# A residual between two layers: squares taken by the scalar engine on transposed rows, and the last three projection tiles run by token halves

## The chip, the cores and the metric

The kernel runs on one core of a Trainium2 chip. The core has a matmul engine (TensorE, PE), a vector engine (VectorE, DVE), a scalar engine (ScalarE, ACT), a general engine (GpSimd, POOL) and a queue engine (SyncE, SP) that issues most of the transfers. Each engine works through its own list of instructions in order; semaphores tie the lists together. The metric is the time of one execution in microseconds (us), smaller is better.

## The reference

Two layers over 528 tokens (16 learned tokens ahead of 512) of width 2048, in float32. Layer 0 is softmax attention, layer 1 gated linear attention (GLA). Around both stands the same frame:

```python
for i in range(DEPTH):                       # DEPTH = 2
    y = rmsnorm(h, pre_norm[i])
    if i % N_MIXERS == 0:
        y = attention_mixer(y, attn_w_in[j], ..., attn_w_out[j], ...)
    else:
        y = gla_mixer(y, gla_w_in[j], gla_gk_up[j], gla_gk_bias[j], gla_o_norm[j], gla_w_out[j])
    h = h + rmsnorm(y, post_norm[i])

def rmsnorm(x, w):
    y = x * rsqrt(mean(x * x, axis=-1) + 1e-6)
    return y * w
```

The change lies between the layers: the output projection of layer 0 (`attn_w_out`), its norm, the residual sum `h + ...`, the norm ahead of layer 1, and the first products of layer 1.

## The kernel before, in words

**Layout.** In this stretch, activations lie transposed: 16 row tiles of 128 features, each with all 528 tokens (T) along the row. Each float32 matmul is made of three cheaper ones: activations and weights are split into a high and a low part (`uh`, `ul`; `whi`, `wlo`), and `three` (L154 to L156) multiplies high by high, low by high and high by low. `split` takes the high part on ACT (L131) and the low part on DVE (L132). Tokens come in two halves of 264 (`HALVES`).

**Weights.** `weights` loads 1024 columns by 128 rows (512 KB) into one of two buffers `wraw`, and splits them into one of three pairs `whi`, `wlo`. A load waits until the split two before it has read its `wraw` buffer; a split waits until PE has used the pair three before it. `project` computes one output tile of 128 features from two such pieces, one token half after the other, each with 16 x 3 matmuls. `group` runs several output tiles at once, contraction step by contraction step, so that it can begin while its input is still being made.

**The stretch.** (1) A `group` computes output tiles 0 and 1 of layer 0's projection while the attention's last rows arrive. Beside it, the weights of GLA's low-rank gate are brought in: `wr` (loaded on POOL's queue, split into `wl`) and `ur`, which has a buffer of its own and is copied into the rows of `ups`. (2) `project` computes tiles 2 to 15. For each half, `squares` takes the output to `hs` (times `post_norm`) and its square on ACT; POOL adds the squares into `acc` (L648). (3) After tile 15, `mean_rsqrt` sums `acc` over the features by a matmul with ones, and makes the scale `r0` (DVE, then a logarithm and an exponential on ACT), per half. (4) `residual(k, a, b)` does row tile k: DVE multiplies `hs` by `r0` (L669), the old `h` (`h0`, reloaded on SP's queue) is added by DVE for even and POOL for odd k (L670), ACT casts the high part times `pre_norm` to `uh` (L671), DVE makes `ul` (L672), ACT squares the new `h` (L677), POOL adds that into `acc` (L678). (5) The next `group` (key tiles of GLA, accumulated in four PSUM banks) calls `low_rank` at each step: that does one residual ahead, multiplies the row tile by `wl` (L691, L692, tile `plr`), transposes it (L698, tile `ht`), copies it (L700, tile `hb`) and stores it for the end of the kernel. The first six row tiles (`NB`) go by halves, the rest whole. (6) `mean_rsqrt` makes the second norm `r1row` from `acc`; it scales what was accumulated (`lt`, `kf`); five transposes turn it into a column `r1col`.

**What sets the order.** The code keeps a model clock (`Clock`): every matmul steps it, and work handed to `clk.after` is written out when the clock gets there. The lists of the engines are then laid out by the framework from that order; weights are drawn ahead (`high_priority`).

Of the kernel before, what the change touches and what calls it, by code (L numbers as in the profile page):

```python
# [82 lines left out]
def hybrid_encoder(  # L83
# [59 lines left out]
    def weights(src, ahead=AHEAD, queue=nc.sync):  # L143
        n = src.shape[-1]
        with tc.high_priority(ahead):
            raw = wpool.tile([P, 1024], F32, tag="wraw", name="wraw", bufs=2)
# [2 lines left out]
            queue.dma_start(out=raw.rearrange("p (k n) -> p k n", n=n), in_=src)
# [480 lines left out]
    nc.gpsimd.dma_start(out=ur, in_=gla_gk_up[0].rearrange("d r n -> r d n"))  # L630
    for t in lrs + [ups]:
        G.memset(t.bitcast(F32), 0.0)
    A.copy(ups[0:16], ur)
# [1 line left out]
    V.tensor_tensor(ups[32:48], ur, ups[0:16].bitcast(F32), op=ALU.subtract)
# [4 lines left out]
    def squares(m, ps, a, b):  # L640
        A.activation(hs[m][:, a:b], ps, AF.Copy, scale=col(POST + m))
        if m == 0:
            A.activation(acc[:, a:b], ps, AF.Square)  # L643
# [20 lines left out]
    def residual(k, a, b):  # L664
        if a == 0:
            h0s[k] = t2.tile([P, T], F32, tag="h0", name="h0", bufs=6)
            nc.sync.dma_start(out=h0s[k], in_=h0_d[k])
# [1 line left out]
        V.tensor_tensor(h, h, r0[:, a:b], op=ALU.mult)  # L669
        (G if k % 2 else V).tensor_tensor(h, h, h0s[k][:, a:b], op=ALU.add)  # L670
        A.activation(hi, h, AF.Copy, scale=col(PRE + KT + k))  # L671
        V.scalar_tensor_tensor(ul[:, k, a:b], h, col(PRE + KT + k), hi.bitcast(F32), op0=ALU.mult, op1=ALU.subtract)  # L672
        if k == 0:
            A.activation(acc[:, a:b], h, AF.Square)
        else:
            sq = t2.tile([P, T], F32, tag="sq1", name="sq1")[:, :b - a]
# [1 line left out]
            G.tensor_tensor(acc[:, a:b], acc[:, a:b], sq, op=ALU.add)  # L678
# [9 lines left out]
    def low_rank(k, part):  # L688
# [4 lines left out]
        if part == 0:  # L693
            return
        ps = (ps_p.tile([P, 512], F32, tag="pp", name="ht") if k % 2 else
              ps_t.tile([P, 512], F32, tag="t", name="ht"))
        for t in range(4):
            PE.transpose(ps[:, t * P:(t + 1) * P], hs[k][:, t * P:(t + 1) * P], ident)  # L698
        hb = t2.tile([P, 512], F32, tag="hb", name="hb")
        A.copy(hb, ps)  # L700
        nc.sync.dma_start(out=h1_d[:, :, k * P:(k + 1) * P].rearrange("t p c -> p t c"),
                            in_=hb.rearrange("p (t c) -> p t c", t=4))
# [31 lines left out]
    lt = tp.tile([P, T], F32, name="lt")  # L734
    for ps, a, b in plr:
        V.tensor_tensor(lt[:, a:b], ps, r1row[:, a:b], op=ALU.mult)
    for i, ps, a, b in banks1:
        take_k(i, ps, a, b)
# [371 lines left out]
```

## Time and profile before

| what | us |
|---|---|
| median of three runs (lowest, highest) | 1824.53 (1823.79, 1826.96) |
| the profiled execution | 1824.21 |
| its span, from first to last instruction | 1822.2 |
| PE busy | 1787.3 (98%) |
| DVE busy | 1014.2 (56%) |
| ACT busy | 891.2 (49%) |
| POOL busy | 204.7 (11%) |

Matmuls overlap, so PE's busy time says only where it had nothing to do. Times in the rows are from the span's start; the stretch of the change lies between about 750 and 1030. In rows, `out<-in` names the tiles, `x2` merges neighbours, and a square bracket gives the idle time ahead of an instruction and who ended it.

### The profile page before, as it was taken

The page shows a single profiled execution, that of the slowest core. Times are in us where ns is not written, and L with a number is a line of the kernel's source. Part 1 is how long each engine was busy: PE and PEld are TensorE (multiplying, and loading weights), DVE is VectorE, ACT ScalarE, POOL GpSimd, SP SyncE. Part 2 cuts the span into 40 slices and gives each one's busy share as a digit, 9 for nine tenths or more (in the row PEclk, how much of TensorE's full clock was granted, in tenths as well). Part 3 has the DMA queues.
Part 4 walks back from the last instruction along what each step waited for, and adds up shares of the span by engine and source line. Part 5 has one row for each costly group of instructions (what it writes and reads, how often), then busy time and mean ns, then how long its engine had stood idle before and what let it go on. Part 6 is the DMA issues. An engine that isn't in the chain of part 4 may idle for free.

```text
span 1822.2 us, 31830 instructions
## 1 busy us (share of the span) xinstructions
PE 1787.3 (98%) x12838; PEld 1685.5 (92%) x12838; DVE 1014.2 (56%) x1942; ACT 891.2 (49%) x1836; POOL 204.7 (11%) x215
## 2 busy tenths in 40 slices
PE   8999999999999999999997999999999999999998
PEld 8899999999999999999987898998999899988886
DVE  5776565656565657622258475656456565654224
ACT  4554544445454545533345586556447554743221
POOL 3211111111111010211137000000000000000000
PEclk9999999999999999999998999999999999999999
DMA  8322323232323332533335323232232333434333
GB/s 268 105 70 74 90 84 87 87 88 84 92 82 91 87 116 81 182 86 93 93 89 162 87 72 90 83 82 82 81 93 76 87 91 88 135 116 167 99 93 127
DMA packets 265955, 184.22 MB, mean 101 GB/s; under 512 B 8188, under 2 KB 241984, under 8 KB 265280
## 3 DMA queue, kind: packets, MB, share of 16 engines
q1 hardware_dynamic: 261152, 165.78, 31.6%
q0 software_dynamic: 4656, 16.42, 2.5%
q8 instruction: 100, 1.64, 0.4%
q14 instruction: 47, 0.39, 0.1%
HBM read 156.03 MB, written 19.64 MB: 96 GB/s over the span
## 4 chain that ended last, share of the span: by engine, by line
PE 91%; DVE 3%; DMA 2%; ACT 1%; issue 1%; POOL 1%; SPq 0%; DVEq 0%; POOLq 0%; ACTq 0%
PE pp L154 22%; PE pp L156 22%; PE pp L155 22%; PE f L1024 2%; PE f L1022 2%; PE f L1023 2%; PE pT L492 2%; PE s L473 1%; PE s L474 1%; PE s L475 1%; PE o L512 1%; PE o L513 1%; PE o L902 1%; PE o L901 1%; PE o L900 1%
## 5 line engine op out<-in xcount | busy, mean ns | idle before, releaser
L154 PE MATMUL pp<-uh,whi 128*128 128x264 f32 (+1 forms) x3072 | 927.2, 302 | 0.7 <-ACT acc L643 0.4
L156 PE MATMUL pp<-uh,wlo 128*128 128x264 f32 (+1 forms) x3072 | 916.5, 298 | 0.3 <-POOL wlo L279 0.3
L155 PE MATMUL pp<-ul,whi 128*128 128x264 f32 (+1 forms) x3072 | 915.0, 298 | 1.2 <-DVE ul L340 1.2
L154 PEld LDWEIGHTS pp<-uh,whi 128*128 128x128 f32 x3072 | 578.1, 188 | 19.6 <-issue 0.8
L155 PEld LDWEIGHTS pp<-ul,whi 128*128 128x128 f32 x3072 | 578.8, 188 | 17.4 <-DVE ul L340 1.8
L156 PEld LDWEIGHTS pp<-uh,wlo 128*128 128x128 f32 x3072 | 578.3, 188 | 16.9 <-POOL wlo L279 0.6
L132 DVE TENSOR_TENSOR wlo<-wraw,whi 128x1024 fp32r<-128x1024 f32 (+1 forms) x257 | 315.5, 1228 | 384.5 <-ACT whi L131 379.2
L131 ACT CAST whi<-wraw 128x1024 fp32r<-128x1024 f32 (+1 forms) x257 | 267.4, 1042 | 416.6 <-PE pp L155 297.1
L482 ACT ACTIVATE pn<-s,mx 128x528 f32<-128x528 f32 (+1 forms) x72 | 50.3, 698 | 88.5 <-DVE mx L479 62.7
L1024 PE MATMUL f<-whi,ul 128*128 128x512 f32 x192 | 75.6, 394 | 0.0
L1022 PE MATMUL f<-whi,uh 128*128 128x512 f32 x192 | 75.5, 393 | 0.0
L1023 PE MATMUL f<-wlo,uh 128*128 128x512 f32 x192 | 75.3, 392 | 0.0
L225 POOL TENSOR_TENSOR qw<-qw,cos 128x528 f32<-128x528 f32 x24 | 31.8, 1327 | 371.5 <-DMA qs<-qw 314.5
L927 POOL DMA_DIRECT2D og_d<-og x24 | 12.9, 543 | 487.2 <-DVE og L925 487.2
L478 DVE TENSOR_REDUCE mx<-s 128x1 f32<-128x528 f32 (+1 forms) x72 | 50.7, 705 | 18.7 <-PE s L475 17.5
L497 DVE TENSOR_TENSOR pl<-pT,ph 128x512 fp32r<-128x512 f32 (+1 forms) x80 | 47.4, 592 | 4.8 <-ACT ph L496 3.8
L235 DVE TENSOR_TENSOR qw<-qw,qs 128x528 f32<-128x528 f32 x24 | 17.0, 707 | 59.1 <-POOL qs L226 59.1
L496 ACT CAST ph<-pT 128x512 fp32r<-128x512 f32 (+1 forms) x80 | 40.6, 507 | 16.0 <-PE pT L492 10.0
L467 POOL TENSOR_TENSOR gs<-gs,gr 128x528 f32<-128x528 f32 x16 | 21.1, 1322 | 220.9 <-ACT gs L141 204.1
L1023 PEld LDWEIGHTS f<-wlo,uh 128*128 128x128 f32 x192 | 36.1, 188 | 8.3
L1024 PEld LDWEIGHTS f<-whi,ul 128*128 128x128 f32 x192 | 36.0, 188 | 8.3
L1022 PEld LDWEIGHTS f<-whi,uh 128*128 128x128 f32 x192 | 36.1, 188 | 8.1
(310 smaller groups left out, 2750.6 us busy)
## 6 DMA issues: line engine op xcount, KB each, us to landing
wraw<-in_gla_w_in_dram SPq DMA_DIRECT2D x96, 512.0 KB, 3.8
wraw<-in_attn_w_in_dram SPq DMA_DIRECT2D x94, 512.0 KB, 3.8
wraw<-in_attn_w_out_dram SPq DMA_DIRECT2D x32, 512.0 KB, 3.9
wraw<-in_gla_w_out_dram SPq DMA_DIRECT2D x32, 512.0 KB, 3.8
qs<-qw SPq DMA_DIRECT2D x96, 66.0 KB, 2.8
h<-h_d SPq DMA_DIRECT2D x16, 264.0 KB, 3.5
h_d<-h POOLq DMA_DIRECT2D x16, 256.0 KB, 3.4
h_d<-hb SPq DMA_DIRECT2D x16, 256.0 KB, 2.8
```

Of the source, the lines that this page charges most:

```text
L131: A.copy(hi, src)
L132: V.tensor_tensor(lo, src, hi.bitcast(F32), op=ALU.subtract)
L154: PE.matmul(ps, wh, uh[:, k, a:b], start=first, stop=False)
L155: PE.matmul(ps, wh, ul[:, k, a:b], start=False, stop=False)
L156: PE.matmul(ps, wl, uh[:, k, a:b], start=False, stop=last)
L478: V.reduce_max(mx, s, axis=AX.XY)
L482: A.activation(pn[:, :T].rearrange("p (a b) -> p a b", a=2), s, AF.Exp, bias=mx, scale=SCALE, accum_out=sm)
L496: A.copy(ph[:, :, c:c + m], pt[:, :, qc:qc + m])
L497: V.tensor_tensor(pl[:, :, c:c + m], pt[:, :, qc:qc + m], ph[:, :, c:c + m].bitcast(F32), op=ALU.subtract)
L1022: PE.matmul(ps, uh[:, k, ts], wh[:, kk], start=(k == 0), stop=False)
L1023: PE.matmul(ps, uh[:, k, ts], wl[:, kk], start=False, stop=False)
L1024: PE.matmul(ps, ul[:, k, ts], wh[:, kk], start=False, stop=(k == KT - 1))
```

## The change

- POOL takes no part in the residual any more: DVE makes all sums with `h0`, and the sum of squares for the second norm comes from ACT. `token_major` transposes four row tiles for 128 tokens into one bank, lets ACT square it with a sum along the row (into `s1`), and for the 512 real tokens copies it and stores it. Tokens now lie on the partitions, so the second norm is a column `r1col` from `s1`; it is spread into `r1row` by five matmuls of ones with a scaled identity (`second_norm`).
- The last three tiles of the projection (`TAIL`) run for token half 1 first and then for half 2, with the same split weights (`kept`; three of the six pieces lie in buffers `own`).
- The residuals of half 1 are put beside the tail's second half (`residuals`), those of half 2 into the group; ten row tiles go by halves in the group. `h0` is loaded by halves into five buffers.
- `ur` loses its own buffer: it is loaded in two parts into the weights' two `wraw` buffers.

The diff, cut to its core:

```diff
-    def weights(src, ahead=AHEAD, queue=nc.sync):
+    def weights(src, ahead=AHEAD, queue=nc.sync, own=None):
...
-    ur = tp.tile([16, 2, 1024], F32, name="ur")
-    nc.gpsimd.dma_start(out=ur, in_=gla_gk_up[0].rearrange("d r n -> r d n"))
     for t in lrs + [ups]:
         G.memset(t.bitcast(F32), 0.0)
-    A.copy(ups[0:16], ur)
-    A.copy(ups[64:80], ur)
-    V.tensor_tensor(ups[32:48], ur, ups[0:16].bitcast(F32), op=ALU.subtract)
+    for d in range(2):
+        ur = wpool.tile([P, 1024], F32, tag="wraw", name="ur", bufs=2)[:16]
+        nc.gpsimd.dma_start(out=ur, in_=gla_gk_up[0, d])
+        A.copy(ups[0:16, d], ur)
+        A.copy(ups[64:80, d], ur)
+        V.tensor_tensor(ups[32:48, d], ur, ups[0:16, d].bitcast(F32), op=ALU.subtract)
...
     def residual(k, a, b):
-        if a == 0:
-            h0s[k] = t2.tile([P, T], F32, tag="h0", name="h0", bufs=6)
-            nc.sync.dma_start(out=h0s[k], in_=h0_d[k])
+        h0 = t2.tile([P, HALF], F32, tag="h0", name="h0", bufs=5)
+        nc.sync.dma_start(out=h0, in_=h0_d[k][:, a:b])
...
-        (G if k % 2 else V).tensor_tensor(h, h, h0s[k][:, a:b], op=ALU.add)
+        V.tensor_tensor(h, h, h0, op=ALU.add)
...
-        if k == 0:
-            A.activation(acc[:, a:b], h, AF.Square)
-        else:
-            sq = t2.tile([P, T], F32, tag="sq1", name="sq1")[:, :b - a]
-            A.activation(sq, h, AF.Square)
-            G.tensor_tensor(acc[:, a:b], acc[:, a:b], sq, op=ALU.add)
...
+        if part != 0 and k % 4 == 3:
+            for i, t in enumerate((2, 3, 4)):
+                clk.after(1.2 + 0.8 * i, lambda t=t: token_major(k - 3, t))
...
+    def token_major(k, t):
+        _, c, n = TOK[t]
+        turn[0] += 1
+        ps = (ps_p.tile([P, 512], F32, tag="pp", name="ht") if turn[0] % 2 and spare[0] else
+              ps_t.tile([P, 512], F32, tag="t", name="ht"))[:n]
+        for j in range(4):
+            PE.transpose(ps[:, j * P:(j + 1) * P], hs[k + j][:, c:c + n], ident)
+        hb = t2.tile([P, 512], F32, tag="hb", name="hb")[:n]
+        A.activation(hb, ps, AF.Square, accum_out=s1[:n, t, k // 4:k // 4 + 1])
+        if t < 4:
+            A.copy(hb, ps)
+            nc.sync.dma_start(out=h1_d[t][:, k * P:(k + 4) * P], in_=hb)
...
-                clk.after(1.5, lambda: mean_rsqrt(r0, [acc[:, a:b], sq], a, b))
-                clk.after(2.5, lambda: ahead(NA))
+                clk.after(2.0, lambda: mean_rsqrt(r0, [acc[:, a:b], sq], a, b))
+                clk.after(3.5, lambda: side.append(clk.drive(residuals())))
...
-    NA, NB = 2, 6
+    TAIL, NB = 3, 10
...
+    def residuals():
+        for k in range(KT):
+            ahead(1)
+            yield 0.6
+            if k % 4 == 3:
+                for t in range(2):
+                    clk.after(2.0 + t, lambda k=k, t=t: token_major(k - 3, t))
+            yield 0.6
...
-    for m in range(2, KT):
+    for m in range(2, KT - TAIL):
         project(w_out0, m * P, HALVES, evac)
+    kept = {}
+    for part in HALVES:
+        for m in range(KT - TAIL, KT):
+            if m not in kept:
+                kept[m] = [weights(w_out0[:, k0:k0 + 8, m * P:(m + 1) * P], own=own.pop(0) if own else None)
+                           for k0 in (0, 8)]
+            project(w_out0, m * P, (part,), evac, ws=kept[m])
...
-    for a, b in HALVES:
-        mean_rsqrt(r1row, [acc[:, a:b]], a, b)
+    def second_norm():
+        V.reduce_sum(r1col, s1, axis=AX.X)
+        V.tensor_scalar(r1col, r1col, 1.0 / D, EPS, op0=ALU.mult, op1=ALU.add)
+        rsqrt_inplace(r1col)
+        for t, c, n in TOK:
+            dg = t2.tile([P, P], F32, tag="dg", name="dg")
+            V.tensor_scalar(dg, ident, r1col[:, t:t + 1], None, op0=ALU.mult)
+            ps = ps_t.tile([P, 512], F32, tag="t", name="mrow")[:, :n]
+            PE.matmul(ps, ones, dg[:, :n], start=True, stop=True)
+            A.copy(r1row[:, c:c + n], ps)
...
+    clk.after(5.0, second_norm)
...
-    for t, c, n in TOK:
-        ps = ps_t.tile([P, 512], F32, tag="t", name="rt")[:n, :P]
-        PE.transpose(ps, r1row[:, c:c + n], ident)
-        V.tensor_copy(r1col[:n, t:t + 1], ps[:, 0:1])
```

Three places show what moves. First POOL's list around the end of layer 0's attention, before the change (`gs` is the gate of the last head, `lr` and `ups` are cleared here):

```order
L467 TENSOR_TENSOR gs<-gs,gr 128x528 x2
L624 DMA wr<-in_gla_w_in_dram 128x16x32
L626 MEMSET wl 128x2048
L630 DMA ur<-in_gla_gk_up_dram 16x2x1024
L632 MEMSET lr_9780 80x528
L632 MEMSET lr_9781 80x528
L632 MEMSET ups 80x2048
```

and with it:

```order
L467 TENSOR_TENSOR gs<-gs,gr 128x528
L633 DMA ur<-in_gla_gk_up_dram 16x1024
L467 TENSOR_TENSOR gs<-gs,gr 128x528
L633 DMA ur<-in_gla_gk_up_dram 16x1024
L630 MEMSET lr_9780 80x528
L624 DMA wr<-in_gla_w_in_dram 128x16x32
L626 MEMSET wl 128x2048
L630 MEMSET lr_9781 80x528
L630 MEMSET ups 80x2048
```

Both `ur` loads, which wait for a `wraw` buffer, now stand ahead of `wr` and the clearing of `wl`. Second, ACT's list at the same place, before (`whi` are splits of weights, `h` and `acc` the evacuation of the first output tile):

```order
L131 CAST whi<-wraw 128x1024
L131 CAST wl<-wr 128x16x16 x2
L131 CAST whi<-wraw 128x1024
L633 CAST ups<-ur 16x2048
L634 CAST ups<-ur 16x2048
L641 ACTIVATE h_9791<-pp,cols 128x264
L643 ACTIVATE acc<-pp 128x264
L131 CAST whi<-wraw 128x1024
```

and with the change:

```order
L131 CAST wl<-wr 128x16x16 x2
L634 CAST ups<-ur 16x1024
L635 CAST ups<-ur 16x1024
L634 CAST ups<-ur 16x1024
L635 CAST ups<-ur 16x1024
L131 CAST whi<-wraw 128x1024
L642 ACTIVATE h_9791<-pp,cols 128x264
L644 ACTIVATE acc<-pp 128x264
L642 ACTIVATE h_9791<-pp,cols 128x264
L131 CAST whi<-wraw 128x1024
```

The two splits for output tile 2, which stood ahead of and between the gate's casts, come after them, the first right behind, the second two evacuations later. Third, DVE's list inside the group of layer 1, before (the numbers tell the row tiles `h` and the buffers of `h0` apart, `r_9808` is `r0`):

```order
L669 TENSOR_TENSOR h_9797<-h_9797,r_9808 128x528
L672 SCALAR_TENSOR_TENSOR ul<-h_9794,cols,uh 128x264
L670 TENSOR_TENSOR h_9797<-h_9797,h_11733 128x528
L672 SCALAR_TENSOR_TENSOR ul<-h_9795,cols,uh 128x264
L672 SCALAR_TENSOR_TENSOR ul<-h_9796,cols,uh 128x264
L669 TENSOR_TENSOR h_9798<-h_9798,r_9808 128x528
L672 SCALAR_TENSOR_TENSOR ul<-h_9797,cols,uh 128x528
L669 TENSOR_TENSOR h_9799<-h_9799,r_9808 128x528
```

and with it, at the start of half 2:

```order
L672 SCALAR_TENSOR_TENSOR ul<-h_9805,cols,uh 128x264
L669 TENSOR_TENSOR h_9791<-h_9791,r_9808 128x264
L669 TENSOR_TENSOR h_9792<-h_9792,r_9808 128x264
L670 TENSOR_TENSOR h_9791<-h_9791,h_11680 128x264
L672 SCALAR_TENSOR_TENSOR ul<-h_9806,cols,uh 128x264
L670 TENSOR_TENSOR h_9792<-h_9792,h_11694 128x264
L669 TENSOR_TENSOR h_9793<-h_9793,r_9808 128x264
L672 SCALAR_TENSOR_TENSOR ul<-h_9791,cols,uh 128x264
```

The sums of every row tile are on DVE's list now, all rows are halves, and half 1 is through (its last row tile is 9806) when half 2 begins.

More of the change, by code (lines that the diff above doesn't have):

```diff
@@ L146, in weights @@
             raw = wpool.tile([P, 1024], F32, tag="wraw", name="wraw", bufs=2)
-            hi = wpool.tile([P, 1024], F32R, tag="whi", name="whi")
-            lo = wpool.tile([P, 1024], F32R, tag="wlo", name="wlo")
+            hi, lo = own or (wpool.tile([P, 1024], F32R, tag="whi", name="whi"),
+                             wpool.tile([P, 1024], F32R, tag="wlo", name="wlo"))
             queue.dma_start(out=raw.rearrange("p (k n) -> p k n", n=n), in_=src)
@@ L644, in squares @@
             return
-        sq = t2.tile([P, 512], F32, tag="sq", name="sq")[:, :b - a]
+        sq = t2.tile([P, HALF], F32, tag="sq", name="sq")
         A.activation(sq, ps, AF.Square)
@@ L692, in low_rank @@
             PE.matmul(ps, wl[:, k, :], ul[:, k, a:b], start=False, stop=(k == KT - 1))
[L693 to L702, printed above, removed]
+        if part != 0 and k % 4 == 3:
+            for i, t in enumerate((2, 3, 4)):
+                clk.after(1.2 + 0.8 * i, lambda t=t: token_major(k - 3, t))
+    s1 = tp.tile([P, 5, 4], F32, name="s1")
+    V.memset(s1, 1.0)
+    def token_major(k, t):
[10 more added lines that the diff above has]
+            nc.sync.dma_start(out=h1_d[t][:, k * P:(k + 4) * P], in_=hb)
+    turn, spare = [0], [True]
     def evac(ps, a, b):
@@ L706, in evac @@
             if a == 0:
-                clk.after(1.5, lambda: mean_rsqrt(r0, [acc[:, a:b], sq], a, b))
-                clk.after(2.5, lambda: ahead(NA))
-            else:
-                clk.after(0.9, lambda: mean_rsqrt(r0, [acc[:, a:b], sq], a, b))
-    NA, NB = 2, 6
-    h0s = {}
-    tasks = [(k, a, b) for a, b in HALVES for k in range(NB)] + [(k, 0, T) for k in range(NB, KT)]
+                clk.after(2.0, lambda: mean_rsqrt(r0, [acc[:, a:b], sq], a, b))
+                clk.after(3.5, lambda: side.append(clk.drive(residuals())))
+            else:
+                clk.after(1.6, lambda: mean_rsqrt(r0, [acc[:, a:b], sq], a, b))
+    TAIL, NB = 3, 10
+    side = []
+    tasks = [(k, a, b) for a, b in HALVES for k in range(KT)]
     def ahead(n):
@@ L719, in ahead @@
                 residual(*tasks.pop(0))
-    for m in range(2, KT):
-        project(w_out0, m * P, HALVES, evac)
+    def residuals():
[6 more added lines that the diff above has]
+            yield 0.6
+    own = [[tp.tile([P, 1024], F32R, name=f"own{i}{w}") for w in "hl"] for i in range(3)]
+    for m in range(2, KT - TAIL):
+        project(w_out0, m * P, HALVES, evac)
+    kept = {}
[5 more added lines that the diff above has]
+            project(w_out0, m * P, (part,), evac, ws=kept[m])
+    clk.finish(*side)
     group([(w_in1, 1024, 256)], accs1, low_rank, halves=NB)
-    for a, b in HALVES:
-        mean_rsqrt(r1row, [acc[:, a:b]], a, b)
+    spare[0] = False
     def take_k(i, ps, a, b):
@@ L732, in take_q @@
         V.scalar_tensor_tensor(qf[:, i, a:b], ps, 1.0 / 16, r1row[:, a:b], op0=ALU.mult, op1=ALU.mult)
[L734 to L738, printed above, removed]
+    lt = r0
+    def second_norm():
[8 more added lines that the diff above has]
+            A.copy(r1row[:, c:c + n], ps)
+        for ps, a, b in plr:
+            V.tensor_tensor(lt[:, a:b], ps, r1row[:, a:b], op=ALU.mult)
+        for i, ps, a, b in banks1:
+            take_k(i, ps, a, b)
+    clk.after(5.0, second_norm)
     project(w_in1, 0, REAL, lambda ps, a, b: take_q(0, ps, a, b))
```

4 lines of the change are left out of this document (2 added, 2 removed).

## The prediction

> **What bounds the kernel now.** I read the page first: TensorE (PE) is busy for 98% of the span, so only its holes can be won. Its row of forty slices shows one broad hole, slices 20 to 22, which is the residual between the layers. Then I read the busy time of each engine by stage (columns: from:to, us, then PE, weight load, DVE, ACT and POOL busy with instruction counts, granted clock, DMA share, GB/s):
>
> ```profile
> 930.00:940.20 10.20, 10.20 (x82) 10.00 (x80) 2.91 (x5) 3.26 (x7) 1.47 (x2) 1.00 0.19 56
> 940.20:1003.20 63.00, 47.11 (x326) 43.85 (x325) 55.81 (x58) 34.86 (x67) 44.93 (x35) 0.92 0.51 148
> 1003.20:1027.00 23.80, 23.80 (x104) 17.47 (x103) 10.88 (x23) 8.73 (x16) 0.00 (x0) 1.00 0.33 88
> ```
>
> Before 940.2 (the projection's end) and after 1003.2 (the group's end) PE has no gap. Between them it is idle for 15.9 us and its clock averages 0.92. What would the stage take without waits? The timeline of PE gives the step from one batch of four transposes (L698) to the next, first where a step holds 8 matmuls (one token half), then where it holds 16; the last two rows are waits:
>
> ```profile
> 954.46 0.60 PE L698 MATMUL ht<-ident,h 128*128 128x128 f32 x4
> 955.90 0.60 PE L698 MATMUL ht<-ident,h 128*128 128x128 f32 x4
> ...
> 998.89 0.60 PE L698 MATMUL ht<-ident,h 128*128 128x128 f32 x4
> 1001.30 0.60 PE L698 MATMUL ht<-ident,h 128*128 128x128 f32 x4
> ...
> 969.57 0.80 PE L698 MATMUL ht<-ident,h 128*128 128x128 f32 x4 [4.42 <-ACT hb L700]
> 991.40 1.11 PE L698 MATMUL ht<-ident,h 128*128 128x128 f32 x4 [2.87 <-ACT hb L700]
> ```
>
> The steps are 1.44 and 2.41 us, so 8 matmuls take 0.97 and a batch of transposes 0.47. The stage has ten steps of 16, six of 8 with a batch and six without: 24.1 + 8.6 + 5.8 = 38.5, and with four matmuls of the first norm, at 8 matmuls' rate and double passes about 0.8, 39.3 us. The excess is 63.0 - 39.3 = 23.7 us. The waits of PE name its cause:
>
> ```profile
> PE ht L698 <- ACT hb L700: 8.2, 4, 4.4
> PE plr L692 <- DVE ul L672: 5.9, 7, 1.5
> ```
>
> ACT had itself been waiting there, for the sums of DVE and POOL. DVE is the bound: it has no pause from 946 to 996 (first row, by stage), but its operations are stretched (rows by line give ns min/median/max and both shapes; then pieces of the timelines):
>
> ```profile
> 946.00:996.00 50.00, 35.87 (x247) 33.28 (x247) 50.00 (x50) 29.13 (x54) 40.12 (x29) 0.91 0.52 152
> ...
> L669 DVE TENSOR_TENSOR h<-h,r x22: 417/697/1839, 937.7 to 985.3; 128x264 f32<-128x264 f32 x12, 128x528 f32<-128x528 f32 x10
> L672 DVE SCALAR_TENSOR_TENSOR ul<-h,cols,uh x22: 480/968/1830, 940.5 to 993.0; 128x264 fp32r<-128x264 f32 x12, 128x528 fp32r<-128x528 f32 x10
> ...
> 935.26 0.61 PE L660 MATMUL ssq<-acc,ones 128*128 128x264 f32 x2
> 937.73 0.78 DVE L669 TENSOR_TENSOR h<-h,r 128x264 f32<-128x264 f32 x2 [0.95 <-ACT r L136]
> 940.46 0.89 DVE L672 SCALAR_TENSOR_TENSOR ul<-h,cols,uh 128x264 fp32r<-128x264 f32 x2
> ...
> 962.41 3.57 DVE L669 TENSOR_TENSOR h<-h,r 128x528 f32<-128x528 f32 x2
> 961.89 1.76 POOL L670 TENSOR_TENSOR h<-h,h 128x528 f32<-128x528 f32 x1 [0.99 <-DVE h L669]
> 963.62 1.80 POOL L678 TENSOR_TENSOR acc<-acc,sq 128x528 f32<-128x528 f32 x1
> ```
>
> Two products of 528 columns took 3.57 us just where POOL ran two of its own for 1.76 and 1.80; two of 264 columns with POOL idle took 0.78.
>
> **The change, part by part.**
>
> 1. *POOL leaves the residual* (its sums of squares and half of the additions). Per half tile DVE then does two sums and one fused operation. Back to back these cost 0.78 - 0.42 = 0.36 twice and 0.89 - 0.48 = 0.41: 1.13 us, or 1.32 if none overlaps. Thirty-two halves make 36 to 42 us instead of the 50 of 946 to 996 that the old share took.
>
> 2. *The last three tiles run first for token half 1, then for half 2.* The first norm of half 1 is ready 4.5 us after its last tile (935.26 to 937.73 is 2.5 behind the norm's matmuls, which are put 2.0 later), while PE still has 3 x 48 matmuls = 17.4 us, one norm and four batches of transposes ahead: 20.0 us. So DVE works for 15.5 us under a full PE; before, it had about 2.5 (937.73 to 940.2).
>
> Call the end of half 1 zero. DVE: 16 halves x 1.13 = 18.1, three weight splits x 1.22 = 3.7, two remaining POOL additions that may block 0.76 each = 1.5: half 1 done at 27.8. The second norm's scale costs about a microsecond, then 18.1 + two splits 2.4: done at 49.3, or at 55 with the upper price on both halves. PE: half 1 of ten row tiles from 20.2 to about 32.5 with its batches and norm, half 2 of the same to 44.5, then six steps of 16 with batches to about 57.5. It needs row tile 9 of half 2 at about 43 (DVE has it at 41), tile 10 at 44.5 (43) and tile 15 at 55.5 (49 to 55). The margin is thin but positive.
>
> 3. *ACT takes the squares.* The rows of its pieces:
>
> ```profile
> L671 ACT ACTIVATE uh<-h,cols 128x264 fp32r<-128x264 f32 x12 | 6.0, 512 | 4.9 <-DVE h L670 2.5 <-POOL h L670 2.3
> L641 ACT ACTIVATE h<-pp,cols 128x264 f32<-128x264 f32 x4 | 1.9, 477 | 8.4 <-PE pp L156 8.4
> L700 ACT COPY hb<-ht 128x512 f32<-128x512 f32 x16 | 9.2, 573 | 6.4 <-PE ht L698 3.7 <-DMA h_d<-hb 2.7
> L1045 ACT ACTIVATE junk<-f x12: 589/598/603, 1723.3 to 1814.0; 128x512 f32<-128x512 f32 x12
> L1045 ACT ACTIVATION_READ_ACCUMULATOR junk<-f x12: 192/194/195, 1723.8 to 1814.5; 128x1 f32 x12
> ```
>
> From zero to the second norm: 32 casts x 0.51 = 16.4; four evacuations of the tail of 0.48 and some 0.38 = 3.4; 20 squares x (0.60 + 0.19) = 15.8; 16 copies x 0.57 = 9.1; five or six splits of about 1.05 = 5.8; small ones 2: 52 us in the 60 that PE takes. It fits only if it seldom waits; before, 34.9 of 63 us were used. The copy's buffer has two slots and is freed by a store, for which ACT once waited 2.7 us; now batches come in threes, and the third reuses the first's slot. Of the 23.7 us I leave 5 as waits (bounds 0 and 12: half of the old excess, since one of the two old blockers is gone).
>
> 4. *Four more batches of transposes* (20 for 16): +1.9 us on PE.
>
> 5. *The second norm becomes a column that is spread back by five matmuls through one PSUM buffer*, each behind a scaling on DVE and ahead of a copy on ACT, with 2 to 4 other matmuls between. The two old norm matmul pairs and five transposes of the row (together about 1.3 us) go. Net +1.5, between 0 and 4; PE never waited there before.
>
> 6. *The small gate matrix ur moves into the two weight buffers.* This is a loss at the start of the projection. Until now it had a place of its own. With the change, the loads of the first projection tile can start only when ur has been read, since they take the same two buffers. The rows (start, us; then landing times):
>
> ```profile
> 754.81 0.38 SPq L149 DMA_DIRECT2D wraw<-in_attn_w_out_dram  x1
> 757.48 1.21 POOL L624 DMA_DIRECT2D wr<-in_gla_w_in_dram  x1
> 761.21 1.22 DVE L132 TENSOR_TENSOR wlo<-wraw,whi 128x1024 fp32r<-128x1024 f32 x1
> 763.11 1.82 POOL L626 MEMSET wl<- 128x2048 f32 x1 [4.42 <-DVE ul L132]
> 764.87 0.54 POOL L630 DMA_DIRECT2D ur<-in_gla_gk_up_dram  x1
> 765.41 1.03 POOL L632 MEMSET lr<- 80x528 f32 x2
> 764.21 4.03 DVE L638 COPY fold<-ident 64x64 f32<-64x64 f32 x2
> 771.04 1.91 ACT L633 CAST ups<-ur 16x2048 fp32r<-16x2048 f32 x1 [0.52 <-DMA ur<-in_gla_gk_up_dram]
> 772.98 2.28 DVE L635 TENSOR_TENSOR ups<-ur,ups 16x2048 fp32r<-16x2048 f32 x1 [1.21 <-ACT ups L633]
> 775.70 0.39 PE L154 MATMUL pp<-uh,whi 128*128 128x264 f32 x1 [0.36 <-ACT acc L643]
> ...
> wraw<-in_attn_w_out_dram SPq DMA_DIRECT2D x10, 512.0 KB, 3.9
> wr<-in_gla_w_in_dram POOLq DMA_DIRECT2D x1, 256.0 KB, 5.6
> ur<-in_gla_gk_up_dram POOLq DMA_DIRECT2D x1, 128.0 KB, 6.1
> ```
>
> POOL's queue issues the second ur load ahead of wr. It waits until the split of 761.21 ends, 762.4; with an issue of 0.54 and one fill of lr of 0.5, wr starts at about 763.5 and lands 5.6 later, at 769.1. ACT casts wl until 769.9 (0.7), then four ur casts of 0.95: the first buffer is free at about 772.1 (DVE's 1.14 after the first cast), the second at 773.9. The tile's first load therefore starts at 772.1 instead of 754.81, lands 3.9 later at 776.0, and is split by 778.3 (1.05 on ACT, 1.22 on DVE). PE resumes at 778.3 instead of 775.7: -2.6 us, between 1 and 7 (the upper end if wr waits for DVE's copies as below). The second half of the weights lands while the first is multiplied. Behind that load on SP's queue stand only further weights.
>
> The ur landing of 6.1 was measured under DVE's copies of 764.21. [...] If wr, too, had to sit out those copies, it would land up to 4.7 us later (768.2 instead of 763.5) and the hole would be 7.3 us; the 6.1 already holds such a time, so I leave it in the bound.
>
> Does PE also come back slower? After the 4.42 and the 2.87 us wait (with short waits just ahead of the second) the clock by stretches was:
>
> ```profile
> 970.00:972.00 2.00, 2.00 (x12) 2.00 (x10) 2.00 (x4) 1.40 (x3) 0.00 (x1) 0.50 0.54 157
> 992.00:994.00 2.00, 2.00 (x11) 2.00 (x10) 2.00 (x2) 2.00 (x4) 1.81 (x2) 0.50 0.48 140
> ```
>
> Half rate for about 3 us each, so 1.7 us lost at a time. A wait of 2.6 lies just under the two, so I add 0.7, less than half of that. [...]
>
> **Sum**, against the profiled execution's 1824.21 us (its span is 1822.2; the median of three runs is 1824.53, 0.3 above, which I neglect): 23.7 - 5 (waits left) - 1.9 (batches) - 1.5 (second norm) - 2.6 - 0.7 (ur) = 12.0 us gained: 1812.2, say 1812.
>
> **The rivals.**
>
> *PE is hardly held at all.* For it: the half-2 margins above, and PE's clean 39.3. Waits 1, second norm 0.5, ur 2: 23.7 - 1 - 1.9 - 0.5 - 2 = 18.3, so 1806.
>
> *The waits change hands.* ACT's 52 us of 60, behind stores with two slots, hold the casts and thereby the matmuls and the transposes, as the 8.2 us row did. With 12 us of waits left, 2.5 for the norm and 4 for ur, 3.3 remain: 1821. It decides where stores take over 3 us to land: then the third batch of each threesome holds ACT for 2 us or more.
>
> *Slower: ACT becomes the bound.* One mechanism, in the same stage: its queue is in order, and each cast behind a waiting copy delays DVE's next fused operation, which delays the next cast. The costs outside the waits are 6.7 (1.9 + 1.5 + 3.3), so 17 us of waits turn the sum negative: ACT's 52 us stretched from 60 to 77, a share of 68%. Before it had 55% (34.86 of 63.00), held by DVE and POOL. At that old share the stage would take 94 us and the kernel about 1841 (23.7 - 34 - 6.7); halfway, at 62%, about 1831. Against it: what held ACT was DVE at the stretched rate, and POOL.
>
> *The change does little of what it says*, because POOL is still in the way: it keeps adding squares of the projection, but only two such additions fall into the residual (1.5 us), which is in the sum.
>
> **How the numbers follow.** Likeliest case (gain 8 to 16, 1808 to 1816) 0.50; hardly held (16 to 21) 0.22; waits change hands (0 to 8) 0.20; slower 0.08. The measurement tells about 0.2%, 3.7 us, from no change; of the third case 0.06 and of the fourth 0.02 lie inside that. Faster 0.86, same 0.08, slower 0.06. The range reaches from the hardly held case's 18.3 and a bit more, 1804, to the third's 1821.
>
> **What the profile of the changed kernel would show.** Right: DVE's products and sums of the residual near 0.4 us with POOL silent; PE full from the first half's norm to the group's end, waits for ul and hb below 6 us together; a hole of 2 to 4 us for the first projection tile near 776. Wrong: PE waiting for ACT's copies or for h_d stores over 10 us; a hole near 776 above 6 us, because the ur loads land late or POOL's queue stalls ahead of wr; or PE waiting at the spread of the second norm for over 4 us.

## The result and the profile after

| kernel | median us (lowest, highest) | ratio to before, 95% interval |
|---|---|---|
| before | 1824.16 (1822.59, 1826.96) | |
| changed | 1809.00 (1808.54, 1809.93) | 0.9916 [0.9899, 0.9933] |
| changed, run again beside other kernels (before there 1824.83) | 1809.81 (1809.02, 1813.63) | 0.9923 [0.9911, 0.9935] |

The kernel became about 15 us faster, where 12 were forecast. The profiled span is 1806.8 us against 1822.2. First the busy times by engine of the changed kernel's page, then who PE waited for between 740 and 1060, then the rows of PE's timeline that stand behind those waits, and the first product after the group (the square bracket is the idle time ahead):

```profile
PE 1784.1 (99%) x12855; PEld 1683.8 (93%) x12855; DVE 1000.9 (55%) x1985; ACT 896.3 (50%) x1869; POOL 163.3 (9%) x185
```

```profile
PE ssq L661 <- issue: 2.5, 1, 2.5
PE pp L154 <- ACT acc L644: 1.0, 1, 1.0
```

```profile
776.90 0.39 PE L154 MATMUL pp<-uh,whi 128*128 128x264 f32 x1 [1.03 <-ACT acc L644]
...
948.17 1.12 PE L661 MATMUL ssq<-acc,ones 128*128 128x264 f32 x2 [2.46 <-issue]
...
986.14 0.60 PE L701 MATMUL ht<-ident,h 128*128 128x128 f32 x4
986.50 0.47 PE L154 MATMUL pp<-uh,whi 128*128 128x512 f32 x1
```

The waits for `ul` (5.9 us) and `hb` (8.2 us) are gone. Three marks split the 15.4 us of the span. The start of the first projection tile moved from 775.70 to 776.90: -1.2. From there to the end of the group it was 227.50 us (to 1003.20) and is 209.24 (to 986.14): +18.3. From the group's end to the program's end it was 819.0 and is 820.7: -1.7, a difference of two single traces over 820 us.

What DVE did in the residual, by operation (count, busy us, mean ns, idle ahead):

```profile
L672 DVE SCALAR_TENSOR_TENSOR ul<-h,cols,uh 128x264 fp32r<-128x264 f32 x32 | 15.4, 504 | 1.6 <-ACT uh L671 1.6
L669 DVE TENSOR_TENSOR h<-h,r 128x264 f32<-128x264 f32 x32 | 13.4, 446 | 1.4 <-ACT r L136 1.4
L670 DVE TENSOR_TENSOR h<-h,h 128x264 f32<-128x264 f32 x32 | 13.2, 428 | 0.0
```

The means are near the shortest instances of before. POOL still had two additions of the projection to do beside them; the second shows how the two engines meet, and it took 2.99 us where the one before took 0.82:

```profile
930.92 0.82 POOL L649 TENSOR_TENSOR acc<-acc,sq 128x264 f32<-128x264 f32 x1 [11.74 <-ACT sq L647]
940.87 2.99 POOL L649 TENSOR_TENSOR acc<-acc,sq 128x264 f32<-128x264 f32 x1 [9.14 <-ACT sq L647]
```

The one large wait that is left, 2.46 us ahead of the second half's norm, has this chain on ACT:

```profile
945.96 0.60 ACT L703 ACTIVATE hb<-ht 128x512 f32<-128x512 f32 x1 [1.61 <-DMA h_d<-hb]
...
946.55 1.03 ACT L131 CAST whi<-wraw 128x1024 fp32r<-128x1024 f32 x1
947.48 0.59 ACT L705 COPY hb<-ht 128x512 f32<-128x512 f32 x1
947.96 0.49 ACT L642 ACTIVATE h<-pp,cols 128x264 f32<-128x264 f32 x1
```

The norm's sum (`ssq`) shares its PSUM buffer with the batches of transposes, and by the code it needs the buffer that the copy at 947.48 empties. The trace names no releaser (`issue`), but the copy ends at 948.07 and PE goes on at 948.17. That copy stands behind a split of weights, and this behind a square that waited 1.61 us for a store to free its slot. PE then ran at half rate for a while (from:to, us, busy by engine, granted clock, DMA share, GB/s):

```profile
948.00:950.00 2.00, 1.83 (x6) 1.56 (x6) 1.66 (x3) 2.00 (x8) 0.00 (x0) 0.57 0.64 214
950.00:952.00 2.00, 2.00 (x11) 1.90 (x11) 1.24 (x3) 1.63 (x6) 0.00 (x0) 0.58 0.65 168
```

That is 2.46 us of idle time and 0.43 x 2 + 0.42 x 2 = 1.7 us of clock.

### The profile page after: what moved, and what is told of

The parts are those of the page before. It is cut to its first block, busy times and chain, and to the rows that moved or that the text cites. A ratio compares the mean times of both kernels' runs of the same rounds, so it can differ in the third digit from the quotient of the medians.

```text
span 1806.8 us, 31956 instructions
## 1 busy us (share of the span) xinstructions
PE 1784.1 (99%) x12855; PEld 1683.8 (93%) x12855; DVE 1000.9 (55%) x1985; ACT 896.3 (50%) x1869; POOL 163.3 (9%) x185
## 4 chain that ended last, share of the span: by engine, by line
PE 92%; DVE 2%; ACT 2%; DMA 1%; POOL 1%; issue 1%; SPq 0%; DVEq 0%; POOLq 0%; ACTq 0%
PE pp L154 22%; PE pp L156 22%; PE pp L155 21%; PE f L1057 2%; PE f L1055 2%; PE f L1056 2%; PE pT L492 2%; PE s L473 1%; PE s L474 1%; PE s L475 1%; PE o L935 1%; ACT whi L131 1%; PE o L934 1%; PE o L933 1%; DMA qs<-qw 1%; PE o L513 1%
## 5 line engine op out<-in xcount | busy, mean ns | idle before, releaser
L154 PE MATMUL pp<-uh,whi 128*128 128x264 f32 (+1 forms) x3024 | 913.4, 302 | 2.1 <-ACT acc L644 1.0
L156 PE MATMUL pp<-uh,wlo 128*128 128x264 f32 (+1 forms) x3024 | 903.1, 299 | 0.4 <-POOL wlo L279 0.3
L155 PE MATMUL pp<-ul,whi 128*128 128x264 f32 (+1 forms) x3024 | 901.4, 298 | 0.3 <-DVE ul L340 0.3
L154 PEld LDWEIGHTS pp<-uh,whi 128*128 128x128 f32 x3024 | 569.1, 188 | 20.7 <-ACT acc L644 1.2
L156 PEld LDWEIGHTS pp<-uh,wlo 128*128 128x128 f32 x3024 | 569.4, 188 | 17.1 <-POOL wlo L279 0.6
L155 PEld LDWEIGHTS pp<-ul,whi 128*128 128x128 f32 x3024 | 569.8, 188 | 16.1 <-DVE ul L340 0.5
L132 DVE TENSOR_TENSOR wlo<-wraw,whi 128x1024 fp32r<-128x1024 f32 (+1 forms) x254 | 310.1, 1222 | 366.1 <-ACT whi L131 360.7
L860 DVE TENSOR_TENSOR eq<-eq,qf 128x512 f32<-128x512 f32 (+1 forms) x56 | 34.4, 614 | 15.7 <-ACT eq L858 14.8
```

What stands on the lines that cost most here:

```text
L132: V.tensor_tensor(lo, src, hi.bitcast(F32), op=ALU.subtract)
L154: PE.matmul(ps, wh, uh[:, k, a:b], start=first, stop=False)
L155: PE.matmul(ps, wh, ul[:, k, a:b], start=False, stop=False)
L156: PE.matmul(ps, wl, uh[:, k, a:b], start=False, stop=last)
```

## The experiments

### Is it POOL? Three kernels

**POOL alone taken out of the kernel before.**

```diff
-        (G if k % 2 else V).tensor_tensor(h, h, h0s[k][:, a:b], op=ALU.add)
+        V.tensor_tensor(h, h, h0s[k][:, a:b], op=ALU.add)
...
-            G.tensor_tensor(acc[:, a:b], acc[:, a:b], sq, op=ALU.add)
```

> The kernel before, with POOL alone taken out of the residual: DVE makes all sums with h0, and POOL's additions of the residual's squares are left out (the second norm is then made from row tile 0's squares alone, its time is the same). Row-major transposes, order of the projection, h0 loads and ur stay as before. Theory P (POOL's share of the time is what held the residual, and nothing else of the change is needed): the excess of about 20 us in the residual stage goes down by half or more, DVE's half tiles near 0.45 us, its span 10 to 16 us below before, 1808 to 1815. Rival O (the new order matters too: residuals of half 1 laid beside the projection's last half, ten row tiles by halves and token-major transposes): under 8 us gained, 1816 to 1822, with PE still waiting for ul and hb by 5 us or more in the group.

Measured: 1805.64 us (1804.10 to 1807.33), ratio 0.9894 [0.9881, 0.9908]. Theory P held, and by more than it said: the edit is worth about 19 us, more than the whole change (it leaves out the sum of the squares, which the change has to make elsewhere). DVE's groups in the residual, and PE's longest wait:

```profile
L672 DVE SCALAR_TENSOR_TENSOR ul<-h,cols,uh 128x528 fp32r<-128x528 f32 x10 | 7.7, 767 | 2.5 <-ACT uh L671 2.5
L670 DVE TENSOR_TENSOR h<-h,h 128x528 f32<-128x528 f32 x10 | 6.8, 699 | 0.0
L669 DVE TENSOR_TENSOR h<-h,r 128x528 f32<-128x528 f32 x10 | 6.7, 698 | 0.0
```

```profile
PE ht L697 <- ACT hb L699: 2.2, 2, 1.3
```

DVE makes twice as many sums as before and is still done earlier: its last `ul` ends at 982.3, where it ended at 994.8 in the kernel before. The new order of halves, the tail and the transposes by tokens are not needed to free the stage; the last are what it costs to have the squares summed without POOL.

**POOL gets every second sum with h0 back, in the changed kernel.**

```diff
-        V.tensor_tensor(h, h, h0, op=ALU.add)
+        (G if k % 2 else V).tensor_tensor(h, h, h0, op=ALU.add)
```

> The changed kernel, but odd row tiles add h0 on POOL again (as before the change); the squares stay on ACT. Theory P (what stretched DVE is POOL working beside it): DVE's products and fused operations near POOL's sums go from 0.42 and 0.48 to 0.8 or more at the median beside them, DVE's stretch of the residual grows by some 5 to 10 us, PE waits for ul or uh by 3 to 8 us: 1812 to 1817. Rival T (the gain is the early start in the tail alone): DVE loses 16 sums of 0.36, PE waits do not grow, 1808 to 1810.

Measured: 1818.65 us (1816.82 to 1820.27), ratio 0.9964 [0.9950, 0.9978]: some 9 to 10 us of the gain are lost. DVE has 16 operations fewer and each of the others is slower; and PE waits again (second fence):

```profile
L672 DVE SCALAR_TENSOR_TENSOR ul<-h,cols,uh 128x264 fp32r<-128x264 f32 x32 | 17.3, 564 | 0.9 <-ACT uh L671 0.9
L669 DVE TENSOR_TENSOR h<-h,r 128x264 f32<-128x264 f32 x32 | 16.4, 546 | 1.4 <-ACT r L136 1.4
L670 DVE TENSOR_TENSOR h<-h,h 128x264 f32<-128x264 f32 x16 | 9.5, 597 | 0.0
```

```profile
PE plr L685 <- ACT hb L705: 3.1, 1, 3.1
PE ht L701 <- ACT hb L705: 2.7, 2, 2.5
PE ssq L661 <- issue: 2.6, 1, 2.6
```

Here POOL's sums are also waited for, so this doesn't yet tell company from dependence.

**POOL works for nobody.** On the version with `TAIL = 1` (next part), with room made by leaving out the third pair `own`, which it doesn't use:

```diff
+    idle = tp.tile([P, HALF], F32, name="idle")
+    V.memset(idle, 0.0)
...
         V.tensor_tensor(h, h, h0, op=ALU.add)
+        G.tensor_tensor(idle, idle, h, op=ALU.add)
```

> TAIL = 1 with one addition of 128x264 on POOL after each sum with h0, into a tile that nobody reads (32 in all, 0.75 us each when alone): POOL is busy as before the change, but no engine waits for it. Theory C (DVE and POOL slow each other down by running at the same time): DVE's half-tile operations rise from 0.43 to 0.5 to 0.7 us in the mean, DVE becomes the bound again, 8 to 16 us more than without, 1816 to 1824. Rival L (what cost time before was waiting for POOL's results, not its company): within 2 us of TAIL = 1, 1807 to 1811.

Measured: 1823.47 us (1821.75 to 1828.39), ratio 0.9997 [0.9988, 1.0006]. The whole gain is gone, and no instruction of another engine reads what these additions make. DVE's and POOL's groups, the busy times of the stage (columns as above), and who PE waited for:

```profile
L672 DVE TENSOR_TENSOR h<-h,r 128x264 f32<-128x264 f32 x32 | 21.6, 702 | 0.9 <-ACT r L136 0.9
L676 DVE SCALAR_TENSOR_TENSOR ul<-h,cols,uh 128x264 fp32r<-128x264 f32 x32 | 20.1, 643 | 0.0
L673 DVE TENSOR_TENSOR h<-h,h 128x264 f32<-128x264 f32 x32 | 15.3, 492 | 0.0
...
L674 POOL TENSOR_TENSOR idle<-idle,h 128x264 f32<-128x264 f32 x32 | 28.2, 880 | 34.4 <-DVE h L673 34.0
```

```profile
940.00:990.00 50.00, 39.31 (x279) 33.63 (x277) 50.00 (x92) 31.60 (x74) 24.86 (x30) 1.00 0.48 146
```

```profile
PE ht L705 <- DVE h L673: 5.9, 12, 1.2
PE plr L690 <- DVE ul L676: 3.4, 5, 1.0
```

DVE is busy all through, as in the kernel before, and PE is held for what DVE makes. Per half tile DVE's three means grow from 0.427 + 0.426 + 0.489 = 1.34 (`TAIL = 1` without POOL) to 1.84, by 0.50, while POOL's addition takes 0.88; from the first norm to the next product the stage went from 47.7 to 62.6 us, 0.47 per half tile. Single operations show it: in the same trace the products of DVE that began at 984.46 and 991.80 took 0.98 us each, while the sums at 989.40, 991.05 and 992.82 took 0.42 to 0.43 and the fused operations at 986.50 and 991.39 took 0.48. POOL's additions, 0.88 in the mean, stretched less: the projection's additions of the same shape took 0.75 at the shortest in the kernel before. How the two engines hold each other up within one operation is not shown; in the changed kernel it was POOL's addition of 940.87 that took 2.99 us, while the two sums that DVE began at 941.00 took 0.77 together, as they do with POOL idle.

### Is it the tail?

**`TAIL = 1`.** Since `project` always runs half 1 of a tile and then half 2, this is the plain order of tiles, with the residuals still laid out as in the changed kernel.

```diff
-    TAIL, NB = 3, 10
+    TAIL, NB = 1, 10
```

> The changed kernel with a tail of one tile instead of three: residuals of half 1 start 5.8 us ahead of the projection's end instead of 17.4. Theory P+T (both parts are needed: DVE has about 45 us of work and PE 41 behind the projection): DVE starts at its work 11.6 us later against PE, the margins of the forecast (2 us at row tile 9 of half 2, up to 6 at 15) cover some, PE waits 6 to 11 us more: 1815 to 1820. Rival (POOL's absence alone carries the gain, DVE at 1.13 us for a half tile is fast enough): within 3 us of 1809.

Measured: 1808.63 us (1805.49 to 1808.95), ratio 0.9906 [0.9892, 0.9919]. My theory fell: without the tail's 15 us of lead the kernel is no slower. DVE and PE run side by side almost without a pause, and PE has one wait of 0.5 us in the stage (busy times of the stage, DVE's last piece of the residual, then rows of PE's waits; the first row of these is the first projection tile):

```profile
940.00:978.00 38.00, 37.70 (x296) 35.49 (x296) 37.71 (x96) 33.02 (x79) 2.24 (x5) 1.00 0.71 208
...
977.06 0.89 DVE L672 SCALAR_TENSOR_TENSOR ul<-h,cols,uh 128x264 fp32r<-128x264 f32 x2
```

```profile
PE pp L154 <- ACT acc L644: 1.2, 1, 1.2
...
PE ht L701 <- ACT hb L705: 0.5, 1, 0.5
```

Most of the reason can be worked out from rows that the prediction had. A half row tile takes PE 0.97 us for its 8 matmuls, and 20 x 0.47 / 32 = 0.29 as its part of the batches: 1.26 us. DVE needs 1.13. In this trace it did the 32 half tiles from 938.22 to 977.95, 39.7 us, with three weight splits (3.7) and the second half's scale (0.4) among them: 1.24 each with these, 1.11 without. Once POOL is out, DVE just keeps ahead of PE in the steady state and needs no more lead than the 2 us that it has here (the projection ends near 940.4). The framework also lays batches of half 1 among PE's first steps, which gives DVE some time; how much of the slack this is, no run tells.

**No kept pieces either, and ur in its own buffer again.**

```diff
+    ur = tp.tile([16, 2, 1024], F32, name="ur")
+    nc.gpsimd.dma_start(out=ur, in_=gla_gk_up[0].rearrange("d r n -> r d n"))
...
-    own = [[tp.tile([P, 1024], F32R, name=f"own{i}{w}") for w in "hl"] for i in range(3)]
-    for m in range(2, KT - TAIL):
+    for m in range(2, KT):
         project(w_out0, m * P, HALVES, evac)
...
```

> The changed kernel without its tail and with ur back in its own buffer: tiles 2 to 15 run in one loop, each for half 1 and then half 2, no pieces are kept, and ur is loaded in one transfer as before. POOL stays out of the residual; residuals, squares on ACT and ten row tiles by halves are as in the changed kernel. Theory Q (the wait at the second half's norm comes from work crowded under the tail, and the hole at the first projection tile from ur in the weights' buffers): both vanish, 1803 to 1807, which is 2 to 5 us less than the changed kernel beside it. Rival N (the tail gives as much as its wait costs, and the hole is set by the order of ACT's casts rather than by ur's place): within 1.5 us of the changed kernel, with waits of 2 us or more at another place.

Measured: 1812.30 us (1811.60 to 1813.34), ratio 0.9932 [0.9918, 0.9945], 2.5 us above the changed kernel beside it by medians, with intervals that overlap. Theory Q fell: the two waits went (half a microsecond is left at the norm), but another came. ACT waits for a store, the casts stand behind it, and PE behind these (ACT's timeline, then PE's):

```profile
965.07 0.60 ACT L702 ACTIVATE hb<-ht 128x512 f32<-128x512 f32 x1 [2.67 <-DMA h_d<-hb]
...
965.65 0.91 ACT L670 ACTIVATE uh<-h,cols 128x264 fp32r<-128x264 f32 x2
```

```profile
966.21 0.39 PE L684 MATMUL plr<-uh,wl 128*128 128x264 f32 x1 [2.34 <-ACT uh L670]
```

**The same with three slots for the copy** (`bufs=3` for `hb`).

> The version without tail and without kept pieces (1812.3 us, PE held for 2.3 us where ACT had waited 2.7 us for a store), with three slots for the copy. Theory S4 (that store costs the 2.3 us and some 1.5 us of half clock): both go, 1807.5 to 1810. Rival S5 (the weight pieces of the group, which come later without kept pieces, hold it): the wait moves to another place and the time stays at 1811 to 1813.

Measured: 1809.25 us (1808.26 to 1811.52), ratio 0.9920 [0.9908, 0.9932]. Theory S4 held: the wait of 2.34 us is gone from the trace, the stage from first norm to next product goes from 53.6 to 50.4 us, and the median falls by 3, though the intervals of the two ratios overlap. This is the prediction's "waits change hands", at its mechanism: some 3 us where it strikes.

**Six row tiles by halves instead of ten** (`NB = 6`, otherwise as the version without tail).

> As the version without tail and with ur in its own buffer, but six row tiles by halves in the group in place of ten, as in the kernel before. From the seventh row tile on the group then needs both halves at once, so half 2 of row tile 6 is due after 12 half steps and not after 20. Theory D (DVE at 1.13 us per half tile is ahead of PE by a few us only): DVE needs half 2's seventh row tile about 4 steps of 1.44 us, some 5 us, earlier than with ten; PE waits 3 to 7 us for ul, 1807 to 1813. Rival W (DVE is so far ahead that six halves do): the same within 1 us as with ten.

Measured: 1811.46 us (1810.10 to 1814.09), ratio 0.9929 [0.9916, 0.9941], within a microsecond of ten; Rival W held. Both kernels also have the same wait behind ACT (2.46 us here, 2.34 with ten), and PE waited for `ul` no more than 0.3 us in either. Six or ten row tiles by halves make no difference here while DVE keeps pace.

### The wait at the norm, and the start

**A third slot for the copy, in the changed kernel** (in `wr`'s memory, which is dead by then).

```diff
-        hb = t2.tile([P, 512], F32, tag="hb", name="hb")[:n]
+        hb = (wr.rearrange("p k n -> p (k n)") if turn[0] % 3 == 0 else
+              t2.tile([P, 512], F32, tag="hb", name="hb"))[:n]
```

> The changed kernel, but every third batch of transposes is copied and stored from a third buffer (the memory of wr, free by then). Theory S (the one PE wait left, 2.46 us ahead of the second norm matmuls of r0, and the half clock behind it come from the store of hb, which frees its slot late: ACT waited 1.61 us for it): the wait on the store at this place goes, the PE wait falls to about 0.9 us, the half clock goes too; 1809.0 - 1.6 - 1.7 = about 1806. Rival Q (ACT is simply behind, with four evacuations, splits and squares in one queue; the store only fills time that ACT would have lost anyway): the PE wait stays above 2 us, time 1808 to 1809.5.

Measured: 1809.95 us (1806.88 to 1812.01), ratio 0.9915 [0.9902, 0.9929]: no change. ACT no longer waits for the store there, but for the next thing in its list, the weights, with the same copy queued behind them (ACT's timeline, then PE's):

```profile
950.27 1.05 ACT L131 CAST whi<-wraw 128x1024 fp32r<-128x1024 f32 x1 [1.50 <-DMA wraw<-in_gla_w_in_dram]
951.22 0.58 ACT L706 COPY hb<-ht 128x512 f32<-128x512 f32 x1
```

```profile
951.90 0.68 PE L661 MATMUL ssq<-acc,ones 128*128 128x264 f32 x2 [2.35 <-issue]
```

The slot was not the cause, only the first of two things that made ACT late at this place.

**ur in four pieces, in memory of its own** (in row tiles of `hs` that are written later).

```diff
+        for c in (0, 512):
+            cs = slice(c, c + 512)
+            ur = hs[12 + 2 * d + c // 512][:16, :512]
+            nc.gpsimd.dma_start(out=ur, in_=gla_gk_up[0, d][:, cs])
+            A.copy(ups[0:16, d, cs], ur)
+            A.copy(ups[64:80, d, cs], ur)
...
```

> The changed kernel, but ur is loaded in four pieces into row tiles hs 12 to 15, which are still free, instead of the two weight buffers. Theory U (the loss at the start of the projection is that the first tile's weights wait for ur's readers): the first load is again issued near 755 us, PE starts that tile within 0.5 us of the group's end, gain 0.7 to 1.2 us: about 1808. Rival (the hole is the evacuation on ACT that stands behind the gate's casts): the wait of 1.0 us stays, no gain.

Measured: 1812.43 us (1811.33 to 1817.64), ratio 0.9936 [0.9923, 0.9950]. The forecast of Theory U failed, but the edit brings a hold of its own and so doesn't test the theory. The weights come early again, yet PE is held 2.37 us, since the evacuation that frees its bank stands behind eight casts on ACT (its timeline, then PE's):

```profile
772.36 0.62 ACT L636 CAST ups<-h 16x512 fp32r<-16x512 f32 x1 [1.25 <-DMA h<-in_gla_gk_up_dram]
...
776.87 0.62 ACT L637 CAST ups<-h 16x512 fp32r<-16x512 f32 x1
777.50 0.48 ACT L644 ACTIVATE h<-pp,cols 128x264 f32<-128x264 f32 x1
777.87 0.38 ACT L646 ACTIVATE acc<-pp 128x264 f32<-128x264 f32 x1
```

```profile
778.31 0.39 PE L154 MATMUL pp<-uh,whi 128*128 128x264 f32 x1 [2.37 <-ACT acc L646]
```

**`TAIL = 1`, with ur in one buffer of its own** (memory of the third pair `own`, which `TAIL = 1` leaves unused).

> The version with TAIL = 1 (tile 15 alone has its pieces kept, which is the plain order of halves), with ur in a buffer of its own and loaded in one transfer again; the memory for it is that of the third pair of buffers, which TAIL = 1 does not use. Theory Q2 (the stage is clean with TAIL = 1, and the hole at the first projection tile comes from ur's place): as TAIL = 1, less 0.5 to 2 us of that hole, 1805 to 1808, a ratio of 0.989 to 0.990. Rival N2 (the hole is set by ACT's casts of ups ahead of the evacuations, wherever ur lies): the hole stays between 0.5 and 2.5 us and the time within 1 us of TAIL = 1, 1807 to 1810.

Measured: 1805.97 us (1804.35 to 1807.19), ratio 0.9901 [0.9888, 0.9915]. The hole at the first projection tile is gone, the largest wait of PE in the stage is 0.9 us. It is the fastest complete kernel of the study, some 3 us below the changed one by medians and by span (1803.9 against 1806.8); the intervals of the two ratios overlap, so this lead is likely, not shown. Against `TAIL = 1` with ur in the weights' buffers the spans are equal (1803.9 and 1803.8), so the worth of the hole itself stays open.

**The same with a third slot for the copy** (in `wr`'s memory).

> As the one before, with a third slot for the copy of the transposes (in wr's memory, which is dead by then). Theory S2 (stores with two slots still hold ACT there, 2.4 us in all with TAIL = 1, but PE has enough ahead): no change within 1 us, ACT's waits for stores gone. Rival S3 (they still cost PE): 1 to 2 us less, 1804 to 1806.

Measured: 1806.34 us (1805.02 to 1808.78), ratio 0.9905 [0.9890, 0.9921]: the same. ACT's waits for stores fall from 2.4 to 1.0 us, and PE has a wait of about a microsecond with and without it. Theory S2 held, except that the waits for stores shrank and did not vanish.

**The changed kernel again**, as the measure for its neighbours:

> The changed kernel once more, unaltered, as the measure for its neighbours in this call. All theories: 1807 to 1811, the wait at the second half's first norm near 2.4 us, the hole at the first projection tile between 1 and 3 us.

Measured: 1809.81 us. The wait at the norm was 3.02 us here, the one at the first projection tile 0.6.

## Why the prediction was right, and where not

**The bound and part 1: right, and shown.** DVE was the bound because its operations were stretched, and POOL's company stretched them. The half tile at 1.13 us came out (means of 0.45, 0.43 and 0.50, which overlap; 1.11 with `TAIL = 1`). Taking POOL out alone gave 19 us; a POOL that nobody waits for took everything away.

**Part 2: wrong.** The margins of 1 to 2 us at row tiles 9 and 10 were counted from the tail's lead, as if it were needed. `TAIL = 1` has no such lead and is as fast. What failed is that the two paces, 1.26 us of PE and 1.13 of DVE per half tile (1.24 with weight splits), were never set against each other. DVE's own schedule came out: in the changed kernel it began its half tiles at 927.81, 4.5 us behind zero by the prediction's count, and ended them at 974.4, which makes 51 us where 49 to 55 were counted. The tail brings a loss of its own: the wait at the norm appears in the changed kernel's runs and in the three of its variants that keep the tail, and in none with `TAIL = 1`. Whether a tail without that wait would be the faster order was not tried.

**Part 3, waits left: right size, partly by luck.** By the prediction's clean stage, the stretch from 776.90 to 986.14 should have gained 23.7 less one batch of 0.5, 23.2; it gained 18.3, so 4.9 was lost where I left 5. Of it 2.5 + 1.7 is the norm's wait, which the prediction didn't name. `TAIL = 1`, with 0.5 us of waits, is also 2.7 us above that clean stage (47.7 against 68.2 - 23.7 + 0.5 = 45.0 from first norm to next product), so the clean stage isn't reached there either, by some 2 us that no wait shows. The old trace says the same: 15.9 us of idle time, and half rate over some 9.5 us of PE's work (970 to 974 and 991 to 997), make 20.6 us and not 23.7. (The four matmul records of the first norm in this stage, set at 0.8 us, took 0.7 there, from 942.57 to 943.26.) So 2 to 3 us of the excess were PE at work, slower than the few steps that I multiplied, and could not be won; the agreement of 4.9 with 5 is partly luck, and these pieces don't add up to the microsecond.

**ACT: not the bound, but the waits run through it.** I counted 52 us of 60, 87%; between 929 and 977 it was busy 36.5 of 48, 76%, less than DVE with 41.6. Where it waited, casts and copies behind it waited too, and this is the form that the large waits left took: the norm, the version without kept pieces, the first projection tile.

**Parts 4 and 5: right sign, likely too dear.** All that follows the group, with the second norm's spread and three of the four batches, takes 1.7 us more, where 1.5 + 1.4 were set. Four executions of the changed kernel differ by 1.4 us among themselves, so the size isn't shown. PE's waits show none for the five matmuls.

**Part 6: right path, too dear.** I put 2.6 + 0.7; the first tile's start moved by 1.2 us, with 1.03 us of idle time, after which the clock stayed at 1.00. These rows of the changed kernel (DVE, ACT and SP's queue) show the path:

```profile
763.89 5.04 DVE L639 COPY fold<-ident 64x64 f32<-64x64 f32 x2
767.76 0.71 ACT L131 CAST wl<-wr 128x256 fp32r<-128x256 f32 x2 [5.58 <-issue]
771.18 20.60 SPq L149 DMA_DIRECT2D wraw<-in_attn_w_out_dram  x7
775.14 1.05 ACT L131 CAST whi<-wraw 128x1024 fp32r<-128x1024 f32 x1 [2.17 <-PE pp L156]
...
776.47 0.38 ACT L644 ACTIVATE acc<-pp 128x264 f32<-128x264 f32 x1
```

The tile's first load was issued at 771.18, once `ur` had been read; I had 772.1. Its split began 3.96 us later, about the 3.9 that such a load takes. (The row names PE as what the split waited for; in the changed kernel with a third slot, which has the same order, the trace names the load, with 2.30 us.) Behind the split in ACT's list stands the evacuation of the group's bank, which ended at 776.85, and PE went on at 776.90. DVE's part of the split was done at 777.45, where I had 778.3: the chain came out as counted, 0.9 us earlier throughout. PE did not wait for all of it either, since two products go by `whi` alone and only the third, at 777.50, needs `wlo`. The case of my upper bound, that `wr` sits out DVE's copies, didn't occur: `wr` had landed by 767.76, while DVE's copies ran from 763.89 to 768.93, and from 763.9 to 767 POOL's queue moved 112 packets, 0.33 MB. In the kernel before it moved none from 764 to 768.5, beside copies of 764.21 to 768.24. That such copies hold a load was not shown, nor were the 7 us.

In runs with the same order of these instructions the idle time was 0.6, 0.6, 1.0, 1.2, 1.4 and 2.8 us, so one trace prices it poorly. The hole comes from the two weight buffers and ACT's order together: `ur` in one buffer of its own with two casts shows no such wait in any of five traces, while other memory in four pieces put eight casts ahead of the evacuation and made it 2.37 us.

## What to carry to other kernels

In this kernel DVE was the bound, and additions given to POOL beside it did not relieve it: with 16 sums given back to POOL its three operations took 43.2 us in the residual, with all sums on DVE 42.0. So compare the shortest and the mean duration of DVE's operations before splitting work, and let POOL run idle once to price its company. Before building a lead for a producer, set its pace against the consumer's in the steady state. And a wait that is removed can show the next one in the engine's list, as ACT's 1.61 us for the store became 1.50 us for the weights with a third slot: look at what stands ahead of the instruction that others need, not only at the wait that the trace names.

## What was not expected of the hardware

Whether PE falls to half rate does not go by the length of its wait alone. The granted clock fell to 0.5 for some 3 us after waits of 2.35 and 2.78 us in the changed kernel with a third slot, 2.34 us in the version without tail, 2.37 us in the one with ur in four pieces, and 2.46 us in the changed kernel; after 3.02 us in the second run of the changed kernel, and after 3.54 us in the one with ur in four pieces, it stayed at 1.00. Even the same length goes both ways: 2.46 us was followed by half rate in the changed kernel, where the matmuls behind it came 0.22 us apart, and by full rate in the version with six row tiles by halves, where they came 0.12 us apart. How long the half rate lasts differs too: after the 2.87 us of the kernel before it lasted until 997, some 6 us, and not the 3 that I read. Here is the wait of 3.02 us (PE's timeline and the stretches, both of the second run of the changed kernel):

```profile
949.53 0.68 PE L661 MATMUL ssq<-acc,ones 128*128 128x264 f32 x2 [3.02 <-issue]
```

```profile
948.00:950.00 2.00, 0.47 (x3) 0.47 (x3) 1.02 (x1) 2.00 (x6) 0.00 (x0) 1.00 0.72 262
950.00:952.00 2.00, 2.00 (x15) 1.81 (x15) 1.85 (x6) 2.00 (x7) 0.00 (x0) 1.00 0.48 149
952.00:954.00 2.00, 2.00 (x19) 2.00 (x18) 1.38 (x4) 2.00 (x7) 0.00 (x0) 1.00 0.96 268
```

What decides, the runs don't tell.
